# Fetching an expert's tokens by indirect DMA and transposing them, in place of products with one-hot matrices

## The chip, the cores and the metric

One NeuronCore of a Trainium2 chip runs the kernel; the metric is the device time of one execution in microseconds. Five engines work side by side, each through its own instructions in a fixed order: PE (TensorE, matmuls and transposes), ACT (ScalarE), DVE (VectorE), POOL (GpSimd) and SP (SyncE, which here only issues DMAs). ACT and POOL issue some DMAs as well. An instruction waits until the data and the buffers that it needs are released by the others, and what stands behind it on the same engine waits with it.

## The reference

Two blocks of a network over 512 tokens of width 1024. The change touches only the last step of the second block, a mixture of 16 experts of which each token uses two:

```python
def hierarchical_moe(h, w_rg, b_rg, w_re, b_re, w1, w3, w2):
    t = h.reshape(b * s, d)                        # 512 tokens x 1024
    p_group = jax.nn.softmax(t @ w_rg + b_rg)      # 4 groups of 4 experts
    g_val, g_idx = lax.top_k(p_group, 1)
    ...
    e_val, e_idx = lax.top_k(jax.nn.softmax(fine_sel, axis=-1), 2)
    ...
    for e in range(16):
        y_e = (jax.nn.silu(t @ w1[e]) * (t @ w3[e])) @ w2[e]     # 1024 -> 512 -> 1024
        out = out + combine[:, e:e + 1] * y_e
    return out
```

`setup_inputs` draws all tensors from normal distributions in float32.

## The kernel before

An expert does not run over all 512 tokens but over 128 slots: the router gives every token a position in each of its two experts (`posx`), and tokens past position 127 are left to a separate loop (`overflow`), which is skipped when there are none.

**Precision.** A product in float32 is made of three products of the faster type float32r: each operand is split into a rounded part and the rest (`xh`, `xl` for tokens, `whi`, `wlo` for weights). `split_raw` makes the weight parts: a cast on ACT (L598), then a subtraction on DVE (L599). `split` does the same for activations (L604, L605). `mm3` issues the three products (L612, L614, L616): first `whi` with `xh`, then `wlo` with `xh`, then `whi` with `xl`. With two outputs of 512 columns, a chunk of weights gives six matmuls: two need `xh` and `whi`, two also `wlo`, and the last two need `xl`.

**Weights.** An expert has 12 chunks of 128x1024 (512 KB each): eight for the way up (`w1` and `w3`), four for the way down. SP loads them through 12 buffers (`braw`); `whi` and `wlo` have three buffers each. So PE, when it has done with a chunk, lets ACT cast the third chunk after it.

**Dispatch.** For a pair of experts, `one_hot_slots` makes on DVE (L2339) the matrix `oh`, which for each of four token tiles says which token sits in which slot of either expert. `gather` multiplies the tokens (kept in two parts `hh` and `hl`, tiles `mhh` and `mhl` in the rows) with it: the result is the transposed token matrix of both experts at once. `dispatch(pr, half)` does this for half of the 1024 features, 32 matmuls of 256 columns, and splits the result into `xh` and `xl`. Pair 0 is begun before the router has finished (`early_dispatch`).

**Order of work.** The loop over `e` in `moe` interleaves neighbours. In turn e: the transposes of expert e-1's activations `e_y` (L2256), chunks 4 to 7 of the way up of expert e, the four chunks down of expert e-1, whose result ACT copies out (`put_y`, L2475) and sends to DRAM (`yd`); then one half of a dispatch (in turns 0 to 13: half 0 of pair e/2+1 in even turns, half 1 in odd ones); then chunks 0 to 3 of the way up of expert e+1. A scheduler may shift neighbouring instructions of an engine; in the program that runs, the order on each engine is fixed. At the end the results are fetched from `yd` by indirect DMA on POOL (L2413) and summed; experts 14 and 15 go back to their tokens by products with `oh`.

Of the kernel before, what the change touches and what calls it, by code (L numbers as in the profile page):

```python
# [11 lines left out]
F32 = mybir.dt.float32  # L12
F32R = mybir.dt.float32r
U32 = mybir.dt.uint32
# [6 lines left out]
P = 128  # L21
# [246 lines left out]
def host_consts():  # L268
    f32 = np.float32
    K = {}  # L270
    i = np.arange(P)
    z = []
    dec = np.zeros((6, P, 512), f32)
    deltas = np.linspace(math.log(1e-2) / 0.3, math.log(1e-2) / 1.5, 512, dtype=f32)
    for n, L in ((0, 512), (4, 256)):
        pos = np.arange(L, dtype=f32)
        t = (pos / f32(L - 1))[:, None]
        f = np.linspace(1e-4, 15, 16, dtype=f32)
        ang = f32(2.0 * math.pi / L) * pos[:, None] * f[None, :]
        z.append(np.concatenate([t, np.cos(ang), -np.sin(ang)], axis=-1).T)  # L280
        dd = np.exp(-t * np.abs(deltas)[None, :]) + f32(0.05)
        dec[n:n + L // P] = (dd * f32(1.0 / L)).reshape(-1, P, 512)
    K["zT"] = np.ascontiguousarray(halves(np.concatenate(z, axis=1).astype(f32)))
    K["dec"] = np.ascontiguousarray(halves(dec.reshape(TOK, 512).T).T.reshape(6, P, 512).transpose(1, 0, 2).astype(f32))
    small = np.zeros((P, 1384), f32)
    o = 0
    small[:, 0:128] = np.eye(P)
    small[:, 128:256] = 1.0
    for b in range(2):
        small[b * 64:(b + 1) * 64, 256 + b * 64:256 + (b + 1) * 64] = 1.0  # L290
    inv = np.full((P, P), NEG, f32)
    dF = np.where(i[:, None] <= i[None, :], 0.0, NEG)
    dB = np.where(i[:, None] >= i[None, :], 0.0, NEG)
    small[:, 512:640] = inv
    small[:, 640:768] = dF
    small[:, 768:896] = dB
    small[:, 896:1024] = inv
    small[:, 1028] = EPS
    small[:, 1040:1104] = np.eye(8).reshape(1, 64)
    small[:, 1104:1120] = np.arange(16) * 128  # L300
    small[:, 1030:1034] = np.arange(4) - 4
    small[:, 384:416] = i[:, None] % 32 == np.arange(32)[None]
    small[:, 416:512] = 0.0
    small[:, 1128:1256] = i[:, None] < i[None, :]
    small[:, 1256:1384] = i[None, :]
    K["small"] = small
    jm = np.zeros((64, TOK), f32)
    seq = {0: np.r_[np.arange(512, 768), np.arange(0, 512)],
           1: np.r_[np.arange(767, 511, -1), np.arange(511, -1, -1)]}
    for d, h, j in GROWS:  # L310
        pos = np.empty(TOK, int)
        pos[seq[d]] = np.arange(TOK)
        tl = np.arange(j * P, (j + 1) * P)
        jm[gate_row(d, h, j)] = (pos >= pos[tl].min())
    K["jmask"] = jm
    sm = np.zeros((64, LAT), f32)
    tt = np.arange(LAT)
    for d in range(2):
        for h in range(8):
            for j in range(4):  # L320
                sm[d * 32 + h * 4 + j] = (tt >= j * P) if d == 0 else (tt < (j + 1) * P)
    K["smask"] = sm
    r = np.repeat(np.arange(8, dtype=f32), 64)
    c = np.tile(np.arange(64, dtype=f32), 8)
    inv = (10000.0 ** (-np.arange(0, 32, 2, dtype=f32) / f32(32))).astype(f32)
    cos = np.zeros((P, LAT), f32)
    sin = np.zeros((P, LAT), f32)
    for p in range(P):
        q = p % 64
        a = (r if q < 32 else c) * inv[q % 16]  # L330
        cos[p] = np.cos(a)
        sin[p] = -np.sin(a) if (q % 32) < 16 else np.sin(a)
    K["rope"] = np.ascontiguousarray(np.stack([cos, sin], axis=1))
    return K
# [209 lines left out]
class KB:  # L544
# [79 lines left out]
    def setup(self):  # L624
        nc, I = self.nc, self.I
        self.psum = self.pool("psum", space=PSUM)
        self.cp = self.pool("consts")
        self.wp = self.pool("weights")
        self.dp = self.pool("dram", space=DRAM)
        self.wbufs = (4, 3)  # L630
        cp = self.cp
        self.cols = cp.tile([P, NCOL], F32, name="cols")
        nc.sync.dma_start(self.cols, I["cols"])
        self.small = cp.tile([P, I["small"].shape[1]], F32, name="small")
        nc.sync.dma_start(self.small, I["small"])
        s = self.small
        self.ident, self.ones, self.blk = s[:, 0:128], s[:, 128:256], s[:, 256:384]
        self.mF, self.mB = s[:, 512:768], s[:, 768:1024]
        self.eps = s[:, 1028:1029]
        self.eps2 = cp.tile([P, 1], F32, name="eps2")  # L640
        nc.vector.tensor_tensor(self.eps2, self.eps, self.eps, OP.mult)
        self.onec = s[:, 128:129]
        self.oh8 = s[:, 1040:1104].rearrange("p (a b) -> p a b", a=8)
        self.e128 = s[:, 1104:1120]
        self.m4 = s[:, 1030:1034]
        self.sel32 = s[:, 384:416]
        self.upper = s[:, 1128:1256]
        self.iota = s[:, 1256:1384]
        self.ones_r = cp.tile([P, P], F32R, name="ones_r")
        nc.vector.tensor_copy(self.ones_r, self.ones)  # L650
        sel = cp.tile([P, 4], F32, name="sel")
        nc.vector.tensor_tensor(sel[:, 0:2], self.ident[:, 0:2], self.ident[:, 64:66], OP.add)
        nc.vector.tensor_tensor(sel[:, 2:4], self.ident[:, 32:34], self.ident[:, 96:98], OP.add)
        self.sel = sel
        cs = cp.tile([P, 16], F32, name="cs")
        nc.scalar.activation(cs, self.col("cc", 0, 16), AF.Silu)
        self.cs = cs
        self.ada = [cp.tile([P, 48, 2], F32, name=f"ada{l}") for l in range(2)]
# [1607 lines left out]
    def moe_setup(self, es):  # L2266

        nc, I = self.nc, self.I
        ip = self.pool("moei", es=es, side="right")
        M = {"sel": ip.tile([P, 4, 16], F32R, name="sel"), "selsum": ip.tile([P, 16], F32R, name="selsum"), "posx": ip.tile([P, 4, 16], F32, name="posx"),  # L2270
             "co": ip.tile([P, 4, 16], F32, name="co"), "wv": ip.tile([P, 2, 4], F32, name="wv"),
             "gidx": ip.tile([P, 2, 4], U32, name="gidx"), "cnt": ip.tile([P, 2], F32, name="cnt"),
             "xt": ip.tile([P, 4, 1024], F32, name="xt"), "wl": ip.tile([P, 2, 4], F32, name="wl"),
             "hh": ip.tile([P, 4, 1024], F32R, name="mhh"), "hl": ip.tile([P, 4, 1024], F32R, name="mhl"),
             "ip": ip}

        M["yd"] = self.dp.tile([LAST + 1, 1024], F32, name="yd")
        zero = ip.tile([8, P], F32, name="zero")
        nc.vector.memset(zero, 0.0)
        nc.gpsimd.dma_start(M["yd"][LAST:LAST + 1].rearrange("o (a b) -> (o a) b", b=P), zero)  # L2280
        M["h2d"] = self.dp.tile([4, P, 1024], F32, name="h2d")
        self.M = M

    def moe_consts(self, mp):
# [11 lines left out]
    def moe_route(self, mp, T, x, after):  # L2296
# [26 lines left out]
        for k_, t in enumerate(T):  # L2323
# [1 line left out]
            nc.vector.scalar_tensor_tensor(h2, x[:, k_], st[:, 1, k_:k_ + 1], self.wf, OP.mult, OP.mult)  # L2325
            nc.scalar.copy(M["hh"][:, t], h2)
            nc.gpsimd.tensor_tensor(M["hl"][:, t], h2, M["hh"][:, t].bitcast(F32), OP.subtract)
            nc.scalar.dma_start(M["h2d"][t], h2)
        lg = M["ip"].tile([P, nt, 20], F32, name="lg", bufs=1)
        for k_ in range(nt):  # L2330
            nc.vector.scalar_tensor_tensor(lg[:, k_], ps[:, 512 + 32 * k_:532 + 32 * k_], st[:, 1, k_:k_ + 1], self.br,
# [31 lines left out]
    def moe(self, rt, early):  # L2363
# [7 lines left out]
            return (mp.tile([P, 512], F32, name="e_y", bufs=1), mp.tile([P, 4, P], F32R, name="e_yh", bufs=1),  # L2371
                    mp.tile([P, 4, P], F32R, name="e_yl", bufs=1))

        def dispatch(pr, half):

            t = slice(0, 4) if pr else slice(2, 4)
            if half == 0:
                oh = mp.tile([P, 4, 2, P], F32R, name="oh", bufs=1) if pr else early[0]
                self.one_hot_slots(oh, pr, t)
                X[pr] = (oh, mp.tile([P, 8, 2, P], F32R, name="xh", bufs=2), mp.tile([P, 8, 2, P], F32R, name="xl", bufs=2))  # L2380
            oh, xh, xl = X[pr]
            ps = self.ps() if pr else early[1][half]
            self.gather(ps, oh, half, t)
            h4 = slice(4 * half, 4 * half + 4)
            self.split(xh[:, h4], xl[:, h4], ps.rearrange("p (k e n) -> p k e n", k=4, e=2))
        dispatch(0, 0)
        dispatch(0, 1)
        E = [self.expert(ws, X[0][1][:, :, 0], X[0][2][:, :, 0], tiles)]
        next(E[0])
        for _ in rt:  # L2390
# [1 line left out]
        for e in range(16):  # L2392
# [5 lines left out]
                n = self.count(M["ip"], M["cnt"])  # L2398
            if 0 < e < 15:
                self.put_y(mp, e - 1, next(E[e - 1]))  # L2400
            if e < 14:
                dispatch(e // 2 + 1, e % 2)
            if e < 15:
                _, xh, xl = X[(e + 1) // 2]
                E.append(self.expert(ws, xh[:, :, (e + 1) % 2], xl[:, :, (e + 1) % 2], tiles))
                next(E[e + 1])

# [81 lines left out]
    def overflow(self, mp, tiles, n, ip, h2d, xt):  # L2489
# [8 lines left out]
        with self.tc.If(n > 0):  # L2498
            nc.gpsimd.dma_start(cod.rearrange("e p t -> p t e"), self.M["co"])
            with self.tc.For_i(0, 16, 1) as e:  # L2500
                nc.sync.dma_start(c, cod[bass.ds(e, 1)].rearrange("e p t -> p (e t)"))
                for t in range(4):
                    nc.sync.dma_start(x, h2d[t])
                    ws = Stream(self, "moe")
                    ws.order = range(12)
                    ws.ap = self.I["moe"].rearrange("(e c) p n -> e c p n", e=16)[bass.ds(e, 1)].rearrange("e c p n -> (e c) p n")
# [45 lines left out]
```

## Time and profile before

| what | value |
|---|---|
| median of three runs (lowest to highest) | 2692.41 us (2689.79 to 2702.47) |
| the profiled execution | 2689.39 us |
| its span, first to last instruction | 2687.6 us |
| mean granted clock of TensorE | 0.973 of full speed |
| PE, DVE, ACT, POOL busy | 95%, 60%, 45%, 9% of the span |
| turns 0 to 13 with a dispatch | 2347 to 2620 us of the span |

The profile gives for each instruction its start, its duration, the idle time of its engine just before it and what ended that idle time. Matmuls are pipelined: one that shows 0.39 us makes room for the next after 0.23 us, so a run of matmuls is timed from the start of the first to the start of what follows. "PEclk" is the granted clock of TensorE, 1.00 for 2.4 GHz and 0.50 for 1.2 GHz.

### The profile page before, as it was taken

What the parts mean: (1) busy time and instruction counts of PE and PEld (TensorE: products, weight loads), DVE (VectorE), ACT (ScalarE), POOL (GpSimd) and SP (SyncE); (2) the same over time, 40 slices, a digit from 0 to 9 for tenths busy, and PEclk for the clock granted to TensorE, in tenths of its full rate; (3) what the DMA queues carried; (4) which work ended last, traced back from release to release, by engine and by line L of the source; (5) the groups of instructions that cost most, each with busy time, mean ns of one, the idle gap of its engine ahead of it and who ended that gap; (6) DMA issues with size and microseconds to landing.
All of it is one profiled execution on the core that took longest, in us unless ns stands there. A gap on an engine that the chain in (4) does not pass through costs nothing. (4 is left out here: it accounts for less than half of the span.)

```text
span 2687.6 us, 34315 instructions
## 1 busy us (share of the span) xinstructions
PE 2543.8 (95%) x13413; PEld 2074.4 (77%) x13413; DVE 1606.5 (60%) x2268; ACT 1212.8 (45%) x1679; POOL 231.8 (9%) x233
## 2 busy tenths in 40 slices
PE   6999996799999999998999999999899999799998
PEld 3888854587888888887888888888777677688886
DVE  5554366776334333446665544446586876888887
ACT  4444454334212121234554423224457765477775
POOL 2001024300000000000000000000200322100002
PEclk9999998799999999998999999999999999899999
DMA  7344484533323232321102233333221554599996
GB/s 270 99 150 152 159 260 158 208 117 94 118 87 124 74 123 88 121 91 62 40 25 70 81 94 101 95 94 102 89 63 31 141 129 157 214 317 331 333 329 230
DMA packets 119235, 377.95 MB, mean 141 GB/s; under 512 B 13368, under 2 KB 25912, under 8 KB 118042
## 3 DMA queue, kind: packets, MB, share of 16 engines
q1 hardware_dynamic: 105098, 335.53, 38.7%
q0 software_dynamic: 4720, 19.28, 2.1%
q10 hardware_dynamic: 9248, 20.87, 2.1%
q8 instruction: 107, 1.75, 0.3%
q14 instruction: 62, 0.51, 0.1%
HBM read 345.76 MB, written 29.87 MB: 140 GB/s over the span
## 5 line engine op out<-in xcount | busy, mean ns | idle before, releaser
L598 ACT CAST whi<-wraw 128x1024 fp32r<-128x1024 f32 x259 | 271.7, 1049 | 679.7 <-PE d L614 644.4
L612 PE MATMUL d<-hh,whi 128*128 128x512 f32 (+1 forms) x1832 | 563.4, 359 | 14.4 <-ACT hh L474 8.3
L599 DVE TENSOR_TENSOR wlo<-wraw,whi 128x1024 fp32r<-128x1024 f32 x259 | 316.7, 1224 | 426.4 <-ACT whi L598 413.4
L614 PE MATMUL d<-hl,whi 128*128 128x512 f32 (+1 forms) x1832 | 566.2, 359 | 2.8 <-DVE hl L605 1.8
L616 PE MATMUL d<-hh,wlo 128*128 128x512 f32 (+1 forms) x1832 | 560.9, 356 | 0.0
L612 PEld LDWEIGHTS d<-hh,whi 128*128 128x128 f32 x1832 | 308.1, 191 | 88.8 <-ACT whi L598 15.5
L616 PEld LDWEIGHTS d<-hh,wlo 128*128 128x128 f32 x1832 | 311.7, 191 | 56.2 <-issue 3.5
L614 PEld LDWEIGHTS d<-hl,whi 128*128 128x128 f32 x1832 | 310.8, 191 | 54.5 <-DVE hl L475 3.2
L599 DVE TENSOR_TENSOR wlo<-braw,whi 128x1024 fp32r<-128x1024 f32 x192 | 233.7, 1231 | 34.4 <-ACT whi L598 17.4
L598 ACT CAST whi<-braw 128x1024 fp32r<-128x1024 f32 x192 | 199.9, 1050 | 52.2 <-PE d L616 52.2
L614 PE MATMUL d<-al,whi 128*128 128x512 f32 (+1 forms) x575 | 178.2, 355 | 0.0
L612 PE MATMUL d<-ah,whi 128*128 128x512 f32 (+1 forms) x575 | 177.2, 354 | 0.0
L616 PE MATMUL d<-ah,wlo 128*128 128x512 f32 (+1 forms) x575 | 176.7, 353 | 0.0
L880 DVE SCALAR_TENSOR_TENSOR xl<-d,ada,xl 128x512 f32<-128x512 f32 (+1 forms) x93 | 66.6, 719 | 129.8 <-PE d L616 125.2
L616 PEld LDWEIGHTS d<-ah,wlo 128*128 128x128 f32 x575 | 97.5, 189 | 17.1 <-issue 0.9
L612 PEld LDWEIGHTS d<-ah,whi 128*128 128x128 f32 x575 | 96.5, 188 | 18.2 <-ACT whi L598 1.7
L614 PEld LDWEIGHTS d<-al,whi 128*128 128x128 f32 x575 | 97.0, 189 | 15.9 <-DVE al L605 0.8
L1440 DVE TENSOR_TENSOR y<-y,d 128x768 f32<-128x768 f32 (+1 forms) x44 | 36.1, 821 | 104.0 <-PE d L616 85.1
L612 PE MATMUL d<-whi,xh 128*128 128x512 f32 x256 | 80.5, 396 | 0.0
L1439 ACT ACTIVATE y<-y 128x768 f32<-128x768 f32 (+1 forms) x44 | 32.5, 739 | 104.0 <-DVE y L926 103.9
L614 PE MATMUL d<-wlo,xh 128*128 128x512 f32 x256 | 79.4, 391 | 0.0
L616 PE MATMUL d<-whi,xl 128*128 128x512 f32 x256 | 79.1, 390 | 0.0
(619 smaller groups left out, 4523.1 us busy)
## 6 DMA issues: line engine op xcount, KB each, us to landing
braw<-moe SPq DMA_DIRECT2D x192, 512.0 KB, 5.2
wraw<-ffn SPq DMA_DIRECT2D x132, 512.0 KB, 3.6
araw<-ada_w SPq DMA_DIRECT2D x90, 512.0 KB, 4.8
wraw<-win SPq DMA_DIRECT2D x30, 512.0 KB, 3.6
wraw<-wout SPq DMA_DIRECT2D x24, 512.0 KB, 6.6
wraw<-win0b SPq DMA_DIRECT2D x16, 512.0 KB, 3.7
wraw<-gate SPq DMA_DIRECT2D x16, 512.0 KB, 4.1
yd<-e_o ACTq DMA_DIRECT2D x14, 512.0 KB, 7.6
```

Source lines behind the costliest of these rows:

```text
L598: nc.scalar.copy(hi, raw)
L599: nc.vector.tensor_tensor(lo, raw, hi.bitcast(F32), OP.subtract)
L612: nc.tensor.matmul(o, ah, bh, start=start, stop=False)
L614: nc.tensor.matmul(o, ah, bl, start=False, stop=False)
L616: nc.tensor.matmul(o, al, bh, start=False, stop=stop)
L880: self.nc.vector.scalar_tensor_tensor(x[:, m], ps, g, x[:, m], OP.mult, OP.add)
L1439: nc.scalar.activation(y, y, AF.Silu)
L1440: nc.vector.tensor_tensor(y, y, u, OP.mult)
```

## The change

Pair 0 is dispatched as before. For the pairs 1 to 7, `fetch(pr)` makes `oh`, multiplies it with a column of token numbers (`token`, new constants in `small`), which gives the token number of each slot, casts these to integers (`idx`) and lets POOL fetch 128 rows of 4 KB per expert from `h2d`, the copy of the normalised tokens in DRAM that the overflow loop already used. The rows land in parts of `hh` that are no longer needed. `turn(pr, i)` transposes the rows of one expert on PE, eight transposes of 128 columns, and splits the whole token matrix of that expert. A fetch stands in the even turns 0 to 12; turn(·, 0) stands in the odd turns 1 to 13, turn(·, 1) in the even turns 2 to 14, each right in front of the way up of the expert whose tokens it prepares.

```diff
+    small[:, 1384:1388] = i[:, None] + P * np.arange(4)
...
+        self.token = s[:, 1384:1388]
...
-        def dispatch(pr, half):
-
-            t = slice(0, 4) if pr else slice(2, 4)
-            if half == 0:
-                oh = mp.tile([P, 4, 2, P], F32R, name="oh", bufs=1) if pr else early[0]
-                self.one_hot_slots(oh, pr, t)
-                X[pr] = (oh, mp.tile([P, 8, 2, P], F32R, name="xh", bufs=2), mp.tile([P, 8, 2, P], F32R, name="xl", bufs=2))
-            oh, xh, xl = X[pr]
-            ps = self.ps() if pr else early[1][half]
-            self.gather(ps, oh, half, t)
+        def fetch(pr):
+
+            oh = mp.tile([P, 4, 2, P], F32R, name="oh", bufs=1)
+            self.one_hot_slots(oh, pr, slice(0, 4))
+            ps = self.ps()
+            for i in range(2):
+                for t in range(4):
+                    nc.tensor.matmul(ps[:, i:i + 1], oh[:, t, i].bitcast(F32), self.token[:, t:t + 1], start=t == 0, stop=t == 3)
+            idx = mp.tile([P, 2], U32, name="idx", bufs=2)
+            nc.vector.tensor_copy(idx, ps[:, 0:2])
+            rows = [M["hh"][:, 2 * (pr % 2) + i].bitcast(F32) for i in range(2)]
+            for i in range(2):
+                nc.gpsimd.indirect_dma_start(rows[i], None, M["h2d"][:, :], IndirectOffsetOnAxis(ap=idx[:, i:i + 1], axis=0))
+            X[pr] = (*pair(oh), rows)
+
+        def turn(pr, i):
+
+            _, xh, xl, rows = X[pr]
+            ps = self.ps()
+            for k in range(8):
+                nc.tensor.transpose(ps[:, k * P:(k + 1) * P], rows[i][:, k * P:(k + 1) * P], self.ident)
+            self.split(xh[:, :, i], xl[:, :, i], ps.rearrange("p (k n) -> p k n", k=8))
...
-            if e < 14:
-                dispatch(e // 2 + 1, e % 2)
+            if e % 2:
+                if e < 15:
+                    turn(e // 2 + 1, 0)
+            else:
+                if e:
+                    turn(e // 2, 1)
+                if e < 14:
+                    fetch(e // 2 + 1)
```

What this does to the order on three engines, at one turn in the middle of the loop (lines of the changed kernel are one or two higher than before: L2399 is the transpose of fetched rows, L2386 the product with token numbers, L2258 the transpose of `e_y`, L606 the subtraction for `xl` and others).

PE before, from the end of the gather (32 matmuls, which follow the last ones of the way down) to the way up of the next expert:

```order
L2352 MATMUL d<-oh,mhl 128x256
L2351 MATMUL d<-oh,mhh 128x256
L2352 MATMUL d<-oh,mhl 128x256
L612 MATMUL d<-whi,xh 128x512 x2
L614 MATMUL d<-wlo,xh 128x512 x2
L616 MATMUL d<-whi,xl 128x512 x2
```

PE now, the same place in an even turn:

```order
L617 MATMUL d<-whi,e_yl 128x512 x2
L2399 MATMUL d<-small,mhh 128x128 x8
L2386 MATMUL d<-small,oh 128x1 x8
L613 MATMUL d<-whi,xh 128x512 x2
L615 MATMUL d<-wlo,xh 128x512 x2
L2258 MATMUL d<-small,e_y 128x128 x4
L617 MATMUL d<-whi,xl 128x512 x2
```

The way up now follows the transposes whose cast makes its `xh`; in an even turn the transposes of `e_y` have moved in front of the first use of `xl`. In an odd turn L2386 and L2258 are not there. Before, the half that the gather had just made was needed only by chunks 4 to 7.

ACT before, around the copy-out of the way down (`e_o`) and the cast of the dispatched tokens (`xh`):

```order
L598 CAST whi<-braw 128x1024 x4
L2475 COPY e_o<-d 128x1024
L598 CAST whi<-braw 128x1024
L2476 DMA yd<-e_o 128x1024
L604 CAST xh<-d 128x1024
L598 CAST whi<-braw 128x1024 x4
```

ACT now, in an even turn:

```order
L599 CAST whi<-braw 128x1024 x4
L2501 COPY e_o<-d 128x1024
L599 CAST whi<-braw 128x1024
L2502 DMA yd<-e_o 128x1024
L605 CAST xh<-d 128x8x128
L605 CAST e_yh<-d 128x512
L599 CAST whi<-braw 128x1024 x7
```

The cast of `xh` has kept its place behind the copy-out and one weight cast.

DVE now, in an even turn (`idx` waits for the products with token numbers; `oh` is already that of the next pair):

```order
L2254 TENSOR_TENSOR e_y<-e_y,d 128x512
L600 TENSOR_TENSOR wlo<-braw,whi 128x1024 x4
L2388 CAST idx<-d 128x2
L2341 TENSOR_TENSOR oh<-small,posx 128x1024
L600 TENSOR_TENSOR wlo<-braw,whi 128x1024
L606 TENSOR_TENSOR xl<-d,xh 128x8x128
L606 TENSOR_TENSOR e_yl<-d,e_yh 128x512
```

Three instructions stand between the fourth weight subtraction and `xl`; in an odd turn only the one weight subtraction.

## Rows read from the trace of the kernel before

**Rows 1.** Stretches: engine busy time, instructions, granted clock, DMA share, GB/s.

```profile
core 0: us, PE busy (x) PEld busy (x) DVE busy (x) ACT busy (x) POOL busy (x), PEclk, DMA share, GB/s
2430.00:2512.00 82.00, 82.00 (x431) 70.26 (x430) 69.42 (x62) 60.97 (x65) 0.00 (x0) 1.00 0.93 333
```

**Rows 2.** Waits of SP's DMA queue, 2320 to 2640: total us, times, longest.

```profile
SPq L591 <- DVE wlo L599: 223.5, 172, 3.9
```

**Rows 3.** Timeline of PE around one dispatch: start, duration, instruction.

```profile
2450.83 0.28 PE L2351 MATMUL d<-oh,mhh 128*128 128x256 f32 x1
...
2454.66 0.63 PE L612 MATMUL d<-whi,xh 128*128 128x512 f32 x2
...
2456.05 0.61 PE L612 MATMUL d<-whi,xh 128*128 128x512 f32 x2
...
2460.13 0.60 PE L2256 MATMUL d<-small,e_y 128*128 128x128 f32 x4
2460.49 0.71 PE L612 MATMUL d<-whi,xh 128*128 128x512 f32 x2
```

**Rows 4.** Timeline of ACT and DVE around the same dispatch.

```profile
2447.16 4.83 DVE L599 TENSOR_TENSOR wlo<-braw,whi 128x1024 fp32r<-128x1024 f32 x4
...
2451.03 1.01 ACT L2475 COPY e_o<-d 128x1024 f32<-128x1024 f32 x1 [0.31 <-PE d L616]
...
2451.94 1.05 ACT L598 CAST whi<-braw 128x1024 fp32r<-128x1024 f32 x1
...
2453.02 1.23 DVE L599 TENSOR_TENSOR wlo<-braw,whi 128x1024 fp32r<-128x1024 f32 x1 [1.04 <-DMA braw<-moe]
...
2454.86 1.02 ACT L604 CAST xh<-d 128x1024 fp32r<-128x1024 f32 x1 [1.87 <-PE d L2352]
2454.86 1.23 DVE L2339 TENSOR_TENSOR oh<-small,posx 128x1024 fp32r<-128x1024 f32 x1 [0.62 <-PE d L2352]
...
2456.01 1.22 DVE L605 TENSOR_TENSOR xl<-d,xh 128x1024 fp32r<-128x1024 f32 x1
```

**Rows 5.** Groups of instructions, 2345 to 2633: the gather's first product.

```profile
L2351 PE MATMUL d<-oh,mhh 128*128 128x256 f32 x224 | 54.3, 283 | 0.0
```

**Rows 6.** Timeline at 2642 and 2648: products of one column with oh, a small copy.

```profile
2642.40 0.95 PE L2423 MATMUL d<-wl,oh 128*128 128x1 f32 x8
2643.21 0.31 PE L2421 MATMUL d<-small,oh 128*128 128x128 f32 x1
...
2648.28 0.15 DVE L2425 COPY wslot<-d 128x1 f32<-128x1 f32 x1
```

**Rows 7.** The indirect DMAs at the end: POOL's time (ns), landing (us).

```profile
L2413 POOL DMA_INDIRECT mhh<-yd,gidx x4: 1062/1344/1822, 2646.7 to 2657.7; - x4
...
DMA to landing us min/median/max: 4.5/5.8/6.6
```

**Rows 8.** A stretch in which SP fills the empty weight buffers.

```profile
2300.00:2305.00 5.00, 3.86 (x12) 3.11 (x12) 3.36 (x3) 0.00 (x0) 0.00 (x0) 0.66 1.02 418
```

**Rows 9.** Timeline of PE: four instructions that it paused before.

```profile
1992.33 0.50 PE L612 MATMUL d<-hh,whi 128*128 128x512 f32 x1 [1.97 <-DVE ptl L605]
...
2200.82 0.45 PE L612 MATMUL d<-gh,xkh 128*64 128x512 f32 x1 [1.38 <-ACT gh L604]
...
2207.43 0.45 PE L614 MATMUL d<-gl,xkh 128*64 128x512 f32 x1 [1.25 <-DVE gl L605]
...
2668.42 0.72 PE L614 MATMUL d<-wlo,e_yh 128*128 128x512 f32 x2 [1.86 <-DVE wlo L599]
```

**Rows 10.** Stretches right behind those four pauses.

```profile
1993.60:1996.80 3.20, 3.20 (x9) 2.50 (x8) 3.20 (x6) 0.76 (x3) 0.00 (x0) 0.50 0.00 0
...
2201.80:2205.00 3.20, 3.20 (x8) 1.53 (x7) 3.17 (x9) 2.25 (x4) 0.00 (x0) 0.50 0.51 164
...
2208.60:2212.00 3.40, 3.40 (x16) 2.77 (x15) 1.76 (x3) 1.52 (x3) 0.00 (x0) 1.00 0.31 122
...
2669.50:2672.70 3.20, 3.17 (x8) 1.94 (x6) 3.17 (x2) 2.27 (x2) 1.11 (x1) 0.50 0.01 3
```

More of the change, by code (lines that the diff above doesn't have):

```diff
@@ L284, in host_consts @@
     K["dec"] = np.ascontiguousarray(halves(dec.reshape(TOK, 512).T).T.reshape(6, P, 512).transpose(1, 0, 2).astype(f32))
-    small = np.zeros((P, 1384), f32)
+    small = np.zeros((P, 1388), f32)
     o = 0
@@ L2280, in moe_setup @@
         nc.gpsimd.dma_start(M["yd"][LAST:LAST + 1].rearrange("o (a b) -> (o a) b", b=P), zero)
-        M["h2d"] = self.dp.tile([4, P, 1024], F32, name="h2d")
+        M["h2d"] = self.dp.tile([4 * P, 1024], F32, name="h2d")
         self.M = M
@@ L2327, in moe_route @@
             nc.gpsimd.tensor_tensor(M["hl"][:, t], h2, M["hh"][:, t].bitcast(F32), OP.subtract)
-            nc.scalar.dma_start(M["h2d"][t], h2)
+            nc.scalar.dma_start(M["h2d"][t * P:(t + 1) * P], h2)
         lg = M["ip"].tile([P, nt, 20], F32, name="lg", bufs=1)
@@ L2372, in tiles, with pair @@
                     mp.tile([P, 4, P], F32R, name="e_yl", bufs=1))
-        def dispatch(pr, half):
-            t = slice(0, 4) if pr else slice(2, 4)
-            if half == 0:
-                oh = mp.tile([P, 4, 2, P], F32R, name="oh", bufs=1) if pr else early[0]
-                self.one_hot_slots(oh, pr, t)
-                X[pr] = (oh, mp.tile([P, 8, 2, P], F32R, name="xh", bufs=2), mp.tile([P, 8, 2, P], F32R, name="xl", bufs=2))
-            oh, xh, xl = X[pr]
-            ps = self.ps() if pr else early[1][half]
-            self.gather(ps, oh, half, t)
+        def pair(oh):
+            return oh, mp.tile([P, 8, 2, P], F32R, name="xh", bufs=2), mp.tile([P, 8, 2, P], F32R, name="xl", bufs=2)
+        def fetch(pr):
[17 more added lines that the diff above has]
+            self.split(xh[:, :, i], xl[:, :, i], ps.rearrange("p (k n) -> p k n", k=8))
+        X[0] = pair(early[0])
+        self.one_hot_slots(early[0], 0, slice(2, 4))
+        for half in range(2):
+            self.gather(early[1][half], early[0], half, slice(2, 4))
             h4 = slice(4 * half, 4 * half + 4)
-            self.split(xh[:, h4], xl[:, h4], ps.rearrange("p (k e n) -> p k e n", k=4, e=2))
-        dispatch(0, 0)
-        dispatch(0, 1)
+            self.split(X[0][1][:, h4], X[0][2][:, h4], early[1][half].rearrange("p (k e n) -> p k e n", k=4, e=2))
         E = [self.expert(ws, X[0][1][:, :, 0], X[0][2][:, :, 0], tiles)]
@@ L2400, in moe @@
                 self.put_y(mp, e - 1, next(E[e - 1]))
-            if e < 14:
-                dispatch(e // 2 + 1, e % 2)
+            if e % 2:
[6 more added lines that the diff above has]
+                    fetch(e // 2 + 1)
             if e < 15:
-                _, xh, xl = X[(e + 1) // 2]
+                _, xh, xl = X[(e + 1) // 2][:3]
                 E.append(self.expert(ws, xh[:, :, (e + 1) % 2], xl[:, :, (e + 1) % 2], tiles))
@@ L2502, in overflow @@
                 for t in range(4):
-                    nc.sync.dma_start(x, h2d[t])
+                    nc.sync.dma_start(x, h2d[t * P:(t + 1) * P])
                     ws = Stream(self, "moe")
```

## The prediction

> **What bounds the kernel now.** I read the stretches first, then the waits, then the timeline of one turn. In the turns with a dispatch PE is never idle and its clock is full [rows 1]. The transfers have room: SP's queue waits for DVE to free weight buffers, not for the transfers [rows 2]. So a turn costs what PE's instructions cost, and the place to look at is what stands between the way down of one expert and the way up of the next. Call T the moment when PE is through with the way down, 2450.83 in the turn shown. The gather runs from T to 2454.66, T+3.83, and the first chunk of the way up, u0, ends at 2456.05, T+5.22 [rows 3]; u0 itself takes 1.39 us. PE does not wait there, because u0 uses the half of the tokens that the dispatch one turn earlier had made; the cast of the new half begins only at T+4.03 [rows 4], beside u0. There are 224 / 16 = 14 such dispatches [rows 5], 14 x 3.83 = 53.6 us.
>
> **What is removed, and what stands in its place.** The gathers go. A turn has eight transposes of 128 columns; four take 0.36 us (2460.13 to 2460.49) [rows 3], so eight take 0.7 to 0.8, I take 0.8. A fetch adds eight products of one column, 0.81 us in the row (2642.40 to 2643.21) [rows 6]. Per turn PE thus does 0.8 + 0.4 us in the mean where it did 3.83. That alone would be 14 x 2.6 = 36 us less. But the order of the changed kernel puts u0 behind transposes that make its own `xh` and `xl`, so the time from T to the end of u0 is now a chain over ACT and DVE. I work it out for the three kinds of turn.
>
> *Odd turns, and turn 14 (8 turns).* ACT, in its fixed order, copies `e_o` out from T+0.20, casts one weight chunk from T+1.11 [rows 4], and only then `xh`. Instructions that queue on ACT start some 0.93 us apart (0.91 for these two), so `xh` starts at T+2.05; the transposes have been done since about T+1.1. The cast takes 1.02 us [rows 4], so PE can begin u0 at T+3.07. Its first four matmuls need no `xl`: 4 x 0.23 = 0.92, to T+3.99. DVE meanwhile does `wlo` of the chunk cast at T+1.11, from T+2.19 as now (2453.02), and 1.2 us later (the spacing of four that took 4.83) starts `xl` at T+3.39, done at T+4.61 [rows 4]. PE waits for it from T+3.99, and the last two matmuls end u0 at T+4.61 + 0.46 = T+5.07. Before it was T+5.22. The 3 us that PE saves are two pauses, 2.0 and 0.6 us long. Without u0 the price is 5.07 - 1.39 = 3.68 us for each.
>
> *Even turns 2 to 10 (5 turns)* have a fetch. The products with token numbers run in the pause, to T+1.6, and cost nothing there; if the pause went, they would cost their 0.81. But DVE waits for them: `idx` at about T+1.9 (a small copy, 0.15 [rows 6]), `oh` for the next pair from T+2.1 (1.23 us [rows 4]), `wlo` from T+3.3, `xl` from T+4.5 to T+5.7. PE starts u0 at T+3.07 as above, does four matmuls and then the four transposes of `e_y`, moved here, 0.36, to T+4.35, and waits for `xl` until T+5.7; u0 ends at T+6.16. Less u0 and the moved transposes that is 4.41 us.
>
> *The rest.* Turn 12 has a fetch but makes no further `oh`: `xl` ends at T+4.61 as in odd turns, the moved transposes fill the wait, and the price is 5.07 - 1.39 - 0.36 = 3.32. Turn 0 has the fetch alone, 0.81.
>
> Sum: 0.8 + 8 x 3.68 + 5 x 4.41 + 3.3 = 55.6 us, against 53.6 before: **+2.0 us**. The error is that of a queue: 0.3 us per chain either way, 14 x 0.3 = 4 us.
>
> **The clock.** PE now pauses in each of 14 turns, where the row of stretches shows none. Four pauses of that size from the trace: 1.97, 1.38, 1.25 and 1.86 us [rows 9]. Behind three of them the granted clock was 0.50, that is 1.2 GHz, for a stretch; behind the one of 1.25 us it stayed at 1.00 [rows 10]. At half clock 8 matmuls of 512 columns took 3.20 us, at full clock 16 took 3.40 [rows 10]: a stretch of that length at half clock loses 1.6 us where work fills it, and less where it falls on a pause, as it partly does in the fetch turns. I take three falls in four, as in the rows, at 1.2 us: 14 x 0.75 x 1.2 = **12.6 us**. Bounds: 0 if the clock stays, 14 x 1.6 = 22 if it falls each time in full.
>
> **The transfers.** What the changed kernel adds is 14 indirect DMAs of 512 KB. POOL does nothing else in these turns; one takes it 1.3 us, and lands 5.8 us after its issue (4.5 to 6.6) [rows 7]. From `idx` at T+2.1 the second one lands by about T+2.1 + 2.6 + 6.6 = T+11.3, and the first is due about 20.7 us after T (one turn), the second one turn later. So they are hidden, with some 9 us to spare. In bytes an expert needs 12 chunks, one result and now one token matrix, 14 x 0.524 = 7.34 MB; over a turn of 20.7 us that is 355 GB/s, against 333 now [rows 1], and the trace has 418 over 5 us while SP fills empty buffers [rows 8]. I take nothing for it; the price if it were not hidden is rival D. The Trainium skill, page "DMA: Bandwidth & Descriptors", section "Specifications", speaks against the change here: it gives about 358 GB/s as the HBM limit of a core, and by it an expert could not take less than 7.34 / 358 = 20.5 us, so that no saving on PE beyond 0.2 us a turn, 3 us in all, could show. The 418 GB/s are above that limit, and the measurement decides; by either figure the sum above stays, since the chain keeps a turn near 20.7 us.
>
> **Sum.** The profiled execution's 2689.4 (span 2687.6 and 1.8 around it) + 2.0 + 12.6 = 2704.0. The two lower of the runs lie 0.4 and 3.0 us above that execution, in the mean 1.7: I predict 2706 for the median. That is 0.5% above the 2692.4 of before, and half a per cent, 13.5 us, is about what a measurement of this kernel can tell from no change.
>
> **Rivals.**
>
> A, the forecast: the chain takes the place of the gather, and the clock falls behind most pauses. 2698 to 2716.
>
> B, not slower: the chain as above, but the clock stays at full speed. For it: one pause of the four shown left it alone [rows 9, 10], and the pauses come in two parts, with four matmuls between. Against it: three of four. It decides from fewer than about five falls in 14. Time: 2689.4 + 2.0 + 1.7 = 2693, 2688 to 2698. The Trainium skill, page "TensorE: Matmul & The Clock Gate", section "HAM oscillation — how this bites in real kernels", warns only of idle gaps that are longer than any pause worked out here. By that rule B would be the outcome; the rows behind 1.38 and 1.86 us disagree, and I hold to them.
>
> C, faster: the cast of `xh` does not wait behind the copy-out and the weight cast. Then it would run from T+1.1 to T+2.1, `xl` would be there at T+3.35, u0 would end at T+3.8, and each turn would save 1.3 us more: 14 x 1.3 = 18 us, about 2675, and with the cast hidden altogether the 36 us above, 2656. Against it: the order on ACT is fixed and has both instructions ahead. For it only that the copy-out may wait less than now.
>
> D, much slower: the fetched rows come late, or the clock stays low from one pause to the next. The rows become the bound if they land more than 9 us later than worked out, which is 1.6 times the longest landing of the rows on top; about half of the slots are empty (512 x 2 / 16 = 64 tokens per expert) and all of these fetch token 0, and the fetch shares the DMA engines with the weights. If the first one of each pair were 5 us late, 7 x 5 = 35 us, 2741.
>
> **Chances.** A 0.60, B 0.18, C 0.11, D 0.11. The range runs over B's and A's times and some way into D, 2689 to 2722; it leaves out C and most of D. Slower by over 0.5% (above 2706): half and a little more of A, 0.34, and D: 0.45. Faster by over 0.5% (below 2679): most of C, 0.10. The rest within, 0.45.
>
> **What would show it.** Right: PE idle in front of L613 in every turn from 1 to 14, ended by ACT's cast L605, about 2.0 us in odd turns and 1.2 in fetch turns; a second wait in front of L617, ended by DVE L606, about 0.6 us in odd turns and 1.3 in turns 2 to 10; the granted clock between 1.2 and 2.4 GHz in the mean of the stretch, near 0.94 (10 or 11 stretches of 3.4 us in 300 us, at half); no wait for the rows in front of L2399; a turn of about 21.7 us on average, where it was 20.65. Wrong: PE without pauses (C), pauses at full clock (B), PE idle in front of L2399 (D), or weight loads that ACT waits for (transfers).

## The result and the profile after

The changed kernel takes 2715.69 us (median of four runs, 2712.71 to 2720.23); the kernel before took 2692.19 in runs beside it. The ratio is 1.0083, with a 95% interval of 1.0058 to 1.0109: slower by 23.5 us. The forecast was 2706 with a range of 2689 to 2722. The profiled execution took 2712.71, its span is 2710.9 us, 23.3 longer than before.

The stretches of the changed kernel come first; the second answers to [rows 1].

```profile
core 0: us, PE busy (x) PEld busy (x) DVE busy (x) ACT busy (x) POOL busy (x), PEclk, DMA share, GB/s
2430.00:2512.00 82.00, 75.08 (x335) 60.74 (x336) 65.14 (x60) 57.91 (x60) 2.61 (x2) 0.96 0.95 334
2512.00:2633.00 121.00, 112.01 (x510) 90.76 (x509) 94.34 (x87) 84.10 (x89) 7.86 (x6) 0.93 0.95 338
```

PE, never idle before, now stands for 7 of 82 us; its clock is no longer full; the transfers move as much as they did. The waits from 2340 to 2660 us (engine, tile and line, what it waited for: us in total, times, longest) say for whom:

```profile
PE d L613 <- ACT xh L605: 19.1, 14, 2.1
...
DVE idx L2388 <- PE d L2386: 10.4, 7, 1.6
PE d L617 <- DVE xl L606: 7.7, 13, 1.6
DVE xt L2482 <- DMA mhh<-yd,gidx: 7.1, 1, 7.1
```

The first and the third are the two waits of the forecast: 14 times for `xh`, 13 times for `xl`. There is no wait for fetched rows in front of the transposes L2399. The last is one that the forecast did not have. In the timeline (start, duration, instruction, idle before and its releaser) an odd turn, 5, looks like this, where [rows 3, 4] had the gather:

```profile
2445.77 1.03 PE L2399 MATMUL d<-small,mhh 128*128 128x128 f32 x8
2445.96 1.01 ACT L2501 COPY e_o<-d 128x1024 f32<-128x1024 f32 x1 [0.31 <-PE d L617]
2446.87 1.05 ACT L599 CAST whi<-braw 128x1024 fp32r<-128x1024 f32 x1
...
2447.82 1.01 ACT L605 CAST xh<-d 128x1024 fp32r<-128x1024 f32 x1
...
2448.89 0.73 PE L613 MATMUL d<-whi,xh 128*128 128x512 f32 x2 [2.09 <-ACT xh L605]
2449.09 1.22 DVE L606 TENSOR_TENSOR xl<-d,xh 128x1024 fp32r<-128x1024 f32 x1
...
2450.37 1.13 PE L617 MATMUL d<-whi,xl 128*128 128x512 f32 x2 [0.28 <-DVE xl L606]
```

and the turn behind it, 6, which has a fetch, like this:

```profile
2468.01 1.03 PE L2399 MATMUL d<-small,mhh 128*128 128x128 f32 x8
...
2468.88 1.84 PE L2386 MATMUL d<-small,oh 128*128 128x1 f32 x16
...
2470.77 0.16 DVE L2388 CAST idx<-d 128x2 uint32<-128x2 f32 x1 [1.61 <-PE d L2386]
2470.84 1.22 DVE L2341 TENSOR_TENSOR oh<-small,posx 128x1024 fp32r<-128x1024 f32 x1
...
2471.14 0.74 PE L613 MATMUL d<-whi,xh 128*128 128x512 f32 x2 [0.41 <-ACT xh L605]
...
2471.97 1.22 DVE L600 TENSOR_TENSOR wlo<-braw,whi 128x1024 fp32r<-128x1024 f32 x1
...
2473.11 1.22 DVE L606 TENSOR_TENSOR xl<-d,xh 128x1024 fp32r<-128x1024 f32 x1
...
2474.38 0.73 PE L617 MATMUL d<-whi,xl 128*128 128x512 f32 x2 [1.60 <-DVE xl L606]
```

Counted by T as in the prediction, PE begins u0 at T+3.12 in the odd turn and waits for `xl` until T+4.60. In the fetch turn the token products last until T+2.7, not T+1.6: the eight products show as 16 entries and 1.84 us. `idx`, `oh`, `wlo` and `xl` queue behind them on DVE, and PE goes on at T+6.37.

The 23.3 us of span lie in three places:

- Turns 1 to 13, from the transposes of turn 1 (2358.75) to those of turn 14 (2643.17), take 284.4 us; before they took 268.9: **+15.6**. With turn 14 (its u0 ends 5.17 us after the way down, before 1.36: +3.8) and turn 0 (a gather of 3.83 us against 1.84 of token products: -2.0) this is +17.4, and it is the part that the prediction worked out as +14.6.
- Behind turn 14's u0 the end takes 62.56 us (2648.34 to 2710.9); before it took 49.47 (2638.13 to 2687.6): **+13.1**, not in the prediction.
- The stages ahead of the experts, whose work the change leaves alone, ended 7.2 us earlier than in the profile of before: **-7.2**. In the profiles of the nine experiments below the first gather product of pair 0 stands between 7.0 us earlier (e7) and 0.5 us later (e8) than in that profile. Up to 2290 us the order of the instructions is the same in the profiles of before, of the changed kernel and of e2, and e2 stands only 0.8 us earlier. So executions differ there by several microseconds without any change; how much of the -7.2 is that, one profile of before cannot tell.

The 13 us show in the timeline of DVE and PE right behind turn 14 (the rows that it waits for were asked for by POOL at 2653.38):

```profile
2649.62 1.23 DVE L600 TENSOR_TENSOR wlo<-braw,whi 128x1024 fp32r<-128x1024 f32 x1 [1.90 <-ACT whi L599]
...
2657.97 1.28 DVE L2482 SCALAR_TENSOR_TENSOR xt<-mhh,wv,xt 128x1024 f32<-128x1024 f32 x1 [7.13 <-DMA mhh<-yd,gidx]
2659.18 3.49 DVE L600 TENSOR_TENSOR wlo<-braw,whi 128x1024 fp32r<-128x1024 f32 x3
...
2660.45 1.22 PE L615 MATMUL d<-wlo,xh 128*128 128x512 f32 x2 [6.96 <-DVE wlo L600]
```

In the kernel before, the same place on DVE looked like this:

```profile
2649.30 1.23 DVE L599 TENSOR_TENSOR wlo<-braw,whi 128x1024 fp32r<-128x1024 f32 x1 [0.86 <-ACT whi L598]
2651.23 1.28 DVE L2456 SCALAR_TENSOR_TENSOR xt<-mhh,wv,xt 128x1024 f32<-128x1024 f32 x1 [0.71 <-DMA mhh<-yd,gidx]
2652.43 0.68 DVE L2252 TENSOR_TENSOR e_y<-e_y,d 128x512 f32<-128x512 f32 x1
```

With the new instructions in the program the scheduler put the first addition of rows fetched from `yd` earlier on DVE: before it stood right in front of the last product for `e_y`, now five `wlo` that PE needs ahead of that product stand behind it. The rows come some 4.6 us after POOL's request, much as before (4.5 us, 2646.71 to 2651.23), but DVE is now ready for the addition 7.1 us ahead of them. So DVE stands, `wlo` behind it, and PE behind that; the stretch that follows runs at half clock:

```profile
2658.80:2665.20 6.40, 4.75 (x11) 3.79 (x12) 5.69 (x6) 1.13 (x2) 5.49 (x4) 0.50 0.90 314
```

### The profile page after: what moved, and what is told of

It reads as the page before. It is cut to its first block, busy times and chain, and to the rows that moved or that the text cites. A ratio compares the mean times of both kernels' runs of the same rounds, so it can differ in the third digit from the quotient of the medians.

```text
span 2710.9 us, 33915 instructions
## 1 busy us (share of the span) xinstructions
PE 2529.9 (93%) x13189; PEld 2052.2 (76%) x13189; DVE 1606.8 (59%) x2275; ACT 1211.8 (45%) x1679; POOL 254.5 (9%) x247
## 5 line engine op out<-in xcount | busy, mean ns | idle before, releaser
L613 PEld LDWEIGHTS d<-ah,whi 128*128 128x128 f32 x575 | 96.2, 188 | 18.1 <-ACT whi L599 1.7
L613 PE MATMUL d<-whi,xh 128*128 128x512 f32 x256 | 86.7, 422 | 19.1 <-ACT xh L605 19.1
L617 PE MATMUL d<-whi,xl 128*128 128x512 f32 x256 | 85.6, 417 | 7.7 <-DVE xl L606 7.7
```

Source lines behind the costliest of these rows:

```text
L613: nc.tensor.matmul(o, ah, bh, start=start, stop=False)
L617: nc.tensor.matmul(o, al, bh, start=False, stop=stop)
```

## The experiments

**The theory** after the result: in the turns the chain transposes, `xh`, `xl` is the price, through what ACT and DVE have queued ahead of it, and through the clock, which falls behind PE's pauses; the rest is the early wait for the rows of `yd`. **The rivals:** the fetched bytes take time from the weights; the transfers would hold the turn near 22 us even without the chain; the falls of the clock belong to the stage and not to the pauses; the end is longer for another reason than that wait.

### e1 and e5: the additions of the rows from yd moved back

```diff
-        nc.vector.tensor_tensor(y, y, pu[:, 512:1024], OP.mult)
+        self.last_y = nc.vector.tensor_tensor(y, y, pu[:, 512:1024], OP.mult).ins
...
+        with self.tc.issue_after(self.last_y):
             for t, i in ((0, 0), (0, 1), (1, 0), (1, 1), (3, 0), (3, 1)):
                 gathered(t, i, pool=t == 3)
```

> The changed kernel with one edit: the additions of the gathered rows to xt (L2482) are placed behind the product e_y*u of expert 15, where most of them stood before the change. Theory (the wait for the rows of yd in front of the first of these additions holds VectorE for 7.1 us, with wlo behind it, and TensorE for 7.0, and the clock falls for 6.8 us): that pause goes, the end from expert 14's first way up shortens from 62.6 to about 50 us, and the time is 2702 us (2699 to 2706) beside 2715.7 for the changed kernel and 2692.2 for the one before. Rival (the end is longer because TensorE comes to it out of step or at a low clock, whatever VectorE's order): 2711 to 2717, with another pause in the same place.

Measured: 2714.76 us, ratio 1.0097 (1.0081 to 1.0114). The forecast of 2702 was missed, and both the time and the new pause are as the rival had them. The first additions no longer wait on DVE, but the wait went over to ACT, where the products for the fourth token tile stand ahead of casts of weights:

```profile
2671.38 1.15 ACT L2479 ACTIVATE e_o<-mhh,wv 128x1024 f32<-128x1024 f32 x1 [7.11 <-DMA mhh<-yd,gidx]
2672.43 1.98 ACT L599 CAST whi<-braw 128x1024 fp32r<-128x1024 f32 x2
```

PE then stands 5.64 us for `whi`. So this run alone cannot tell the theory from the rival. e5 takes the products for that tile out of e1's list and adds a second edit for them, with `self.last_w` set to ACT's last product of `weighted`:

```diff
+        with self.tc.issue_after(self.last_w):
+            for i in range(2):
+                gathered(3, i, pool=True)
```

> The kernel of e1_tail, in which the wait of 7.1 us for the rows of yd had only gone over from VectorE to ScalarE (its products e_o of the fourth token tile stood ahead of casts of weights), with those two products placed behind the last cast of expert 15's outputs. Theory (that wait in front of work that the weights need, on whichever engine, is the 13 us that the end is longer): no pause of 5 us or more is left behind turn 14, the end from turn 14's transposes shortens from 62.6 to 50 to 53 us, and the time is 2702 us (2698 to 2707). Rival (the end is longer for another reason): another wait of 5 us or more takes its place, 2711 to 2717.

Measured: 2702.13 us (2696.68 to 2705.46), ratio 1.0045 (1.0031 to 1.0060). PE's longest pause behind turn 14's u0 is now this one:

```profile
2685.56 2.33 PE L2466 MATMUL d<-xh,back 128*128 128x512 f32 x9 [2.26 <-PEq L2528]
```

It waits there for its own sequencer (PEq). The end behind turn 14's u0 takes 47.2 us (2649.74 to 2696.9; this is the length that was 62.6, counted from the end of u0 and not, as the expectation has it, from the transposes). Against the runs of before beside each, +23.5 became +11.3, 12.2 us less. The early wait is shown to be the 13 us, within the spread of the runs: on DVE as on ACT it held the weights behind it.

### e2: the changed kernel without its fetches

This kernel leaves the indirect DMAs out, so the transposes take whatever the buffers hold, and its output is not the network's.

```diff
-            for i in range(2):
-                nc.gpsimd.indirect_dma_start(rows[i], None, M["h2d"][:, :], IndirectOffsetOnAxis(ap=idx[:, i:i + 1], axis=0))
```

> The changed kernel without its 14 indirect transfers: the transposes take whatever rows the buffers hold, so that the fetch itself is left out of the computation; all other instructions keep their order. Theory (the longer turns come from the wait for xh and xl and from the clock; the rows are there before they are wanted): the turns stay at 22.0 to 22.2 us and the time is 2712 to 2719 us. Rival (the 7.3 MB of fetched rows take time from the weights, in a stage that moves 335 GB/s): up to 7.3 MB / 335 GB/s = 22 us less, 2694 us, with the waits for xh and xl as long as they were but fewer waits elsewhere.

Measured: 2719.3 us (2709.71 to 2721.24), ratio 1.0099 (1.0077 to 1.0122), at the upper end of the theory's range and far from the rival's 2694. Turns 1 to 12 take 21.65 to 22.3 us, much as with the fetches, and the two waits of PE are the same:

```profile
PE d L613 <- ACT xh L605: 19.2, 14, 2.1
PE d L617 <- DVE xl L606: 8.4, 11, 1.6
```

The 7.3 MB cost nothing here that these runs can tell: between 2360 and 2590 us 312 GB/s were moved in place of 335, and the turns stayed as long.

### e3 and e6: xh ahead of the copy-out on ACT, xl ahead of idx and oh on DVE

```diff
-            if 0 < e < 15:
-                self.put_y(mp, e - 1, next(E[e - 1]))
+            pd = next(E[e - 1]) if 0 < e < 15 else None
...
+            if pd is not None:
+                with self.tc.issue_after(self.cast):
+                    self.put_y(mp, e - 1, pd)
```

Here `self.cast` is the cast to `xh` in `turn`, which now stands ahead of the call of `put_y`, the copy-out; on DVE `xl` moves up with it. e3 has e1's edit too, e6 that of e5.

> The kernel of e1_tail with one edit more: in each turn the copy of expert e-1's output to e_o (0.91 us on ScalarE) and one cast of a weight (whi) no longer stand ahead of the cast of the transposed tokens (xh), and xl stands ahead of wlo and of idx on VectorE. Theory (TensorE waits for ScalarE's queue, then for VectorE's): in odd turns the wait for xh falls from 2.09 to about 1.1 us and the one for xl to nothing (the transposes of e_y cover it); in even turns the products with the token numbers cover xh, and the wait of 1.6 us for xl goes too. Turns of 20.0 to 20.8 us in place of 22.0 to 22.2, some 1.5 us a turn or 20 us in all, and 2682 us (2676 to 2690): faster than before the change by some 10 us. Rival (weights cannot come sooner than at the 335 GB/s of now, 7.4 MB a turn, so that waits for weights take the place of the ones that go): turns stay near 22 us and the time near that of e1_tail (2699 to 2706).

Measured: 2674.05 us (2669.2 to 2674.42), ratio 0.9941 (0.9924 to 0.9957), just below the expected range. In turn 5 the order on ACT and the wait of PE are:

```profile
2437.53 1.05 ACT L599 CAST whi<-braw 128x1024 fp32r<-128x1024 f32 x1 [0.30 <-PE d L617]
2438.49 1.01 ACT L2401 CAST xh<-d 128x1024 fp32r<-128x1024 f32 x1
2439.39 1.02 ACT L2506 COPY e_o<-d 128x1024 f32<-128x1024 f32 x1
...
2437.34 1.03 PE L2399 MATMUL d<-small,mhh 128*128 128x128 f32 x8
2439.55 0.73 PE L613 MATMUL d<-whi,xh 128*128 128x512 f32 x2 [1.18 <-ACT xh L2401]
```

and the stretches of an odd turn and of the fetch turn behind it:

```profile
2437.34:2456.60 19.26, 18.08 (x85) 14.73 (x84) 16.67 (x16) 15.23 (x16) 0.00 (x0) 1.00 1.00 374
2456.60:2476.11 19.51, 19.51 (x101) 16.46 (x100) 17.89 (x18) 15.23 (x16) 3.54 (x2) 1.00 1.02 393
```

One cast of a weight still stands ahead of `xh`; it is the copy-out that moved behind it. The pause that is left is 1.18 us, as expected, and in the fetch turn there is none. The turns are 19.3 and 19.5 us, below the 20.0 to 20.8 of the expectation. For the odd turns that had counted the waits but not that the clock would stay full with them gone: 20.7 us, as turns 1 and 13 of the changed kernel have it, less the 1.5 us that it counted for the waits is 19.2. The chain's queueing on ACT and DVE, which this edit changes together, is shown to be the cost in the turns, and the weights come at 374 and 393 GB/s when they are asked for, so the rival that holds the turn at 22 us falls. e3 still has a pause of 6.7 us behind turn 14, much like e1's.

> The kernel of e3_cast_tail with the same edit to the two products e_o as in e5_tail_both. Theory: its turns stay at 19.3 to 19.8 us, its pause of 6.7 us behind expert 15's first products goes, and the time is 2667 us (2663 to 2671) in place of 2674. Rival (the pause moves on): 2672 to 2676.

Measured: 2667.63 us (2664.04 to 2674.98), ratio 0.9928 (0.9899 to 0.9957), as expected; turns of 19.3 to 19.8, and the longest pause of the end is 2.62 us.

### e4 and e8: each expert's tokens one turn ahead

```diff
+        fetch(1)
...
-            if e % 2:
-                if e < 15:
-                    turn(e // 2 + 1, 0)
-            else:
-                if e:
-                    turn(e // 2, 1)
-                if e < 14:
-                    fetch(e // 2 + 1)
+            if e < 14:
+                turn((e + 2) // 2, e % 2)
+            if e % 2 and e < 12:
+                fetch(e // 2 + 2)
```

> The changed kernel with the transposes, xh and xl of each expert made one turn earlier (and the fetches as much earlier), so that no product waits for them; the additions to xt stand about where they stood before the change. Theory (the chain of transposes, xh and xl is the whole cost, and nothing else holds the stage): no wait for xh or xl is left, TensorE's own work sets the turn, 18.1 to 18.8 us by its 16.4 us of products for an expert, 1.0 of transposes, 0.8 for half of the products with token numbers and some for e_y, and the time is about 13 x 2.2 us under the kernel before: 2660 to 2668 us. Rival (the transfers set it: 7.4 MB a turn; at the 335 GB/s of now that is 22 us a turn and no gain beyond the tail's, 2700; at the 418 GB/s that the stage ahead of this one showed it is 17.7 us and no bound): waits for weights appear in front of L612 to L617 and the time lies between 2668 and 2700, with turns that move more than 350 GB/s.

Measured: 2662.37 us (2660.79 to 2667.15), ratio 0.9900 (0.9884 to 0.9917), as expected. A turn without and one with a fetch:

```profile
2422.39:2440.39 18.00, 18.00 (x86) 14.63 (x85) 16.44 (x16) 15.03 (x16) 0.00 (x0) 1.00 1.01 399
2440.39:2460.11 19.72, 19.72 (x102) 16.46 (x101) 17.64 (x18) 15.22 (x16) 2.62 (x2) 1.00 1.01 376
```

PE is not idle in them and its clock is full, as in [rows 1], but a turn is 18.9 us in the mean where it was 20.65. The page of the Trainium skill that the prediction weighed, "DMA: Bandwidth & Descriptors", also says, in the section "Measured (HBM→SBUF, 128 partitions, SWDGE, issued from GpSimd)", that some 358 GB/s is the share of a core when its neighbour streams as well, and that a core alone reached 425. The 376 to 399 GB/s of these turns, on one core alone, agree with that, and not with the reading of 358 as a limit.

e8 makes the token products cheaper, with two equal columns of token numbers in fp32r, and takes e5's edit for ACT:

```diff
-                    nc.tensor.matmul(ps[:, i:i + 1], oh[:, t, i].bitcast(F32), self.token[:, t:t + 1], start=t == 0, stop=t == 3)
+                    nc.tensor.matmul(ps[:, 2 * i:2 * i + 2], oh[:, t, i], tok[:, t], start=t == 0, stop=t == 3)
```

> The kernel of e4_ahead with two edits: the products with the token numbers use the one-hot matrix as it is (fp32r, two equal columns) in place of fp32 with one column, and the two products e_o stand behind expert 15's last cast, as in e5_tail_both. Theory (in e4 turns with a fetch took 19.73 us and those without 18.0, so that the token products are 1.7 us of TensorE's own time, and nothing else holds it): turns with a fetch fall to 18.5 to 19.0 us, 7 to 8 us in all, the end changes by less than 2 us, and the time is 2654 us (2650 to 2658). Rival (by now the transfers or VectorE set the turn, at 390 GB/s and 90% of the time): turns with a fetch stay above 19.4 and the time above 2659.

Measured: 2655.15 us (2651.66 to 2658.86), ratio 0.9868 (0.9842 to 0.9894), the fastest kernel here, 35.7 us under the one before. Turns with a fetch take 19.0 us, so the token products are 0.7 us cheaper there; the turns without one stay at 18.1:

```profile
2442.37:2461.40 19.03, 19.03 (x93) 15.65 (x92) 17.68 (x18) 15.21 (x16) 2.60 (x2) 1.00 1.02 390
2461.40:2479.48 18.08, 18.08 (x85) 14.72 (x84) 16.45 (x16) 15.01 (x16) 0.00 (x0) 1.00 1.01 399
```

19.03 is just outside the expected 18.5 to 19.0, and 0.7 us in six turns is 4 us of the 8 by which e8 gains more than e4 (35.7 against 27.6 us, each against the runs of before beside it). The rest isn't pulled apart.

### e7 and e9: work in PE's pauses

```diff
+            if i == 0:
+                ps = self.ps()
+                for k in range(7):
+                    nc.tensor.matmul(ps[:, 0:512], M["hl"][:, 0, 0:P], M["hl"][:, 1, 0:512], start=True, stop=True)
```

> The changed kernel with seven products of 512 columns more in each odd turn, right behind the eight transposes, into a buffer that nobody reads: 1.5 us of work in the pause of 2.09 us before xh. Theory (the clock falls behind these pauses, because TensorE stands, and each fall costs 1.5 to 1.6 us: turns 3, 5, 7, 9 and 11 took 22.2 to 22.3 us, turns 1 and 13 without a fall 20.7): the chain stays as it was, the pause shrinks to some 0.6 us, no stretch at 0.50 begins in an odd turn, odd turns take 20.7 us, and the time falls by 5 x 1.55 = 8 us to 2708 us (2705 to 2712), although the kernel does more work. Rival (the fall is tied to the stage and not to the pause): odd turns stay at 22.2 and the time at 2713 to 2719.

Measured: 2717.59 us (2710.52 to 2723.67), ratio 1.0112 (1.0082 to 1.0142): no gain. The same two turns, 5 and 6, first of the changed kernel, then of e7:

```profile
2445.77:2468.01 22.24, 19.87 (x85) 15.79 (x84) 16.85 (x16) 15.31 (x16) 0.00 (x0) 0.92 0.92 308
2468.01:2489.97 21.96, 19.95 (x102) 16.57 (x101) 18.07 (x18) 15.43 (x16) 2.61 (x2) 1.00 0.99 362
```

```profile
2448.13:2468.31 20.18, 19.71 (x92) 15.94 (x91) 16.94 (x16) 15.41 (x16) 0.00 (x0) 1.00 0.95 334
2468.31:2492.44 24.13, 22.57 (x101) 18.44 (x100) 18.07 (x18) 15.42 (x16) 2.61 (x2) 0.86 0.94 330
```

In the odd turn all went as expected: the pause is 0.47 us, the clock stays full, the turn takes 20.2. But the fall came in the fetch turn instead, and there it lasted 6.8 us in place of 3.4: 24.1 us. Half of the theory is borne out: with the pause filled, none of the seven odd turns has a fall, where five had one. The other half, that each pause makes or spares its own fall, is wrong: five of the six fetch turns now have 6.8 us at 0.50. e9 puts five more such products in front of the wait for `xl` in the fetch turns:

```diff
+                for w in (wh, wl):
+                    for o in range(2):
+                        nc.tensor.matmul(pu[:, 512 * o:512 * o + 512], xh[:, k], w[:, 512 * o:512 * o + 512], start=w is wh, stop=False)
+                fill(5)
...
```

> The kernel of e7_filler, whose odd turns fell to 20.2 us without a clock fall while its turns with a fetch rose to 24.1 us with 6.8 us at 0.50 each, with five such products more in the turns with a fetch, where TensorE waits 1.6 us for xl. Theory (a fall follows from TensorE standing somewhere in the pair of turns; with the odd pause filled it came behind the waits of the fetch turn instead): with both filled no stretch at 0.50 begins between 2360 and 2600 us, odd turns stay at 20.2, turns with a fetch take 21.9 to 22.2 as in the changed kernel (their waits are the chain's), a pair 42.2 in place of 44.3, and the time is some 6 x 2.1 = 12 us under the changed kernel's: 2704 us (2699 to 2709). Rival (the falls follow the stage, whatever TensorE does in its waits): falls stay or move once more, and the time is 2712 to 2722.

Measured: 2705.41 us (2697.91 to 2711.97), ratio 1.0060 (1.0032 to 1.0089). Against the runs of before beside each, +23.5 became +17.2. The two intervals overlap, but in the profiles turns 1 to 13 took 278.2 us where the changed kernel's took 284.4, 6.2 us less though PE does more work. Its turn 4 with a fetch, and turns 5 and 6:

```profile
2421.70:2444.16 22.46, 21.14 (x106) 17.39 (x105) 18.05 (x18) 15.32 (x16) 2.61 (x2) 1.00 0.96 358
...
2444.16:2464.37 20.21, 19.74 (x93) 15.95 (x91) 16.95 (x16) 15.42 (x16) 0.00 (x0) 1.00 0.92 331
2464.37:2487.16 22.79, 22.38 (x106) 18.65 (x105) 18.05 (x18) 15.32 (x16) 2.61 (x2) 0.93 0.95 351
```

The odd turns stay at 20.2 with a full clock. Of the six fetch turns four still have one stretch of 3.4 us at 0.50, so the expected "none" did not come, and the fetch turns take 22.5 to 23.1 us, not 21.9 to 22.2. What PE does in its waits does move the clock; why four falls stayed is open.

## Why the prediction was right, and where it was off

The forecast case A came: slower, by two waits that take the place of the gather and by the clock. By its steps:

**The chain, odd turns: right.** u0 was to begin at T+3.07 and end at T+5.07; where the clock stayed full (turns 1, 13 and 14) it did at T+3.12 and T+5.17. Turns 1 and 13 take 20.71 and 20.65 us: as long as before. e3 shows that the order in the queues makes this price. Rival C, the cast of `xh` ahead of the copy-out, is what e3 built by hand: `xh` starts at T+1.15 there where C had T+1.1, and the turns are 1.3 us shorter than before in the mean. That the time of 2674 hits C's 2675 is partly luck, since e3 still has its pause at the end.

**The chain, fetch turns: mis-sized.** The step was "eight products of one column, 0.81 us in the row". The row counts entries of the trace, of which each such product leaves two, so that [rows 6] show four products; eight take 1.84 us, as the line of L2386 above has it. That is 1 us too little in turn 0 and some 0.85 us too little in each chain through `idx`: in turn 6 u0 ends at T+6.94 and not T+6.16, and fetch turns take 21.7 to 22.2. In turn 12, too, `idx` holds `wlo` and `xl`, which the prediction did not count: u0 ends at T+6.61, partly at half clock, and not at T+5.07. The chain costs +9.6 us where the prediction had +2.0, and most of the difference lies in the turns with a fetch.

**The clock: right in kind, too high in size.** 10.5 falls at 1.2 us, 12.6, were predicted. There were eight stretches of 3.4 us at 0.50 in turns 1 to 14. Five stand in odd turns, which took 22.2 to 22.3 us, 1.55 more than the two without: 7.8 us. The three in fetch turns cost next to nothing, since they lie on the wait for `xl`. The four pauses of [rows 9] were a small pick: in the whole trace of before some 28 pauses of 1.0 to 2.2 us begin at full clock, and a fall begins in 16 of them or within 3 us behind, a share nearer to the 8 in 14 turns than to three in four. The Trainium skill's rule on idle gaps ("TensorE: Matmul & The Clock Gate", section "HAM oscillation — how this bites in real kernels"), by which B would have come, does not cover this: no pause in these turns is over 2.09 us, and the clock fell.

**The transfers: right.** There is no wait for rows, and e2 shows no cost of them. They land 5.9 to 8.9 us after their issue, against 4.5 to 6.6 in [rows 7], well inside the spare time. (The 9 us to spare are 1.4 times the longest landing of the rows, not 1.6.) D did not come.

**The end: missed.** The +13.1 us behind turn 14 had no step in the prediction. The change put no instruction there, but the scheduler's order moved, which a comparison of the two orders shows: the first `xt` addition on DVE stood right in front of the last product for `e_y` and now stands in front of five `wlo` as well. The prediction worked with the order around the dispatches alone.

So 17.4 us in place of 14.6 for the turns, 13.1 unforeseen, and -7.2 from stages that the change leaves alone. That the turns came so close is partly luck: the chain was put 7.6 us too low and the clock 4.8 us too high. The forecast of 2706 lies 10 us under the 2715.7; the range held because it reached towards D, not because the end was foreseen, and the -7.2 helped.

**Where the expected gain is.** PE's saving was real, but 36 us was too much, by the same token products: with 0.87 us for the transposes (start to start in turn 6) and 1.84 for a fetch the sum is 53.6 - 14 x 0.87 - 7 x 1.84 = 28.5 us. It needs the two casts to be off the path: with the chain one turn ahead (e4) the kernel is 27.6 us faster than before. The 36 us of e8 come from cheaper token products and the edit of the end on top.

## What to carry over

A product that is replaced by less work of the same engine gains only if what feeds the next product does not stand in other engines' queues: count from the moment at which the engine is through to the moment at which its next operand is there, in the order in which the queues stand, or make the operand one iteration earlier. After an edit of a scheduled kernel, read the order of every engine to its end, above all where an instruction waits for a DMA, since a wait moved ahead of urgent work can cost more than the edit, and moving it off one engine can put it on another. Here a pause often cost more than its length, because the clock fell behind it, so the gain of removing one shows in the granted clock too.

## What the runs showed of the hardware

- Eight fp32 products of one column with a 128x128 operand took 1.84 us, 0.23 us each, as two entries each; with fp32r and two columns turns became 0.7 us shorter.
- With PE's odd pause filled (e7) the fall of the clock moved to the next turn and doubled, from 3.4 to 6.8 us, although that turn's own pauses were no longer than before; it did so in five of the six fetch turns. With a single pause of 1.18 us in each odd turn and none in the fetch turns (e3, e6) the clock stayed at 1.00 through all turns.
- Weights, results and fetched rows together moved 376 to 399 GB/s for whole turns (e4, e8) when PE asked for them, with the DMA share at 1.01 to 1.02, where the kernel before drew 333 [rows 1].
